# Attention times values: the last three two-head units in 4-value pieces with attn stationary, in a fixed order

The chip is a Trainium2; the kernel runs on one of its cores. The metric is device time in microseconds (us) of one execution, of which several are taken.

## The reference

```python
batch, n_heads, seq, head_dim = 8, 12, 1024, 64
attn_weights: float32 [8, 12, 1024, 1024]
v:            float32 [8, 12, 1024, 64]
out = einsum('bhqs,bhsd->bhqd', attn_weights, v)      # float32
```

The attention matrix is 403 MB and is read once. The matmul contracts over s, which lies along the rows of attn in memory, so each block of attn has to be transposed on the chip first.

## The kernel before

Work is cut into 48 *units* of two heads. A unit's attn sits in one tile of 128 partitions (2 heads x 64) and 16 *values* `g`; one value is 128 rows of attn, 64 queries of each head, with all 1024 keys. Loading converts float32 to bf16. Unit 47 is the last one.

Terms used below: PE is the tensor engine and PEld its loading of the stationary operand, DVE the vector engine, ACT the scalar engine, POOL the GpSimd engine, which issues the loads of attn, SP the sync engine, which issues the stores. The *granted clock* is the share of full speed at which PE runs, 1.00 being full. Tiles: `abf` is attn as loaded, `pt` its transposes, `at` their copy, `vbf` v, `po` the results of wide matmuls, `ot` their copy, `px` the results of direct matmuls, of transposes back and of `spread_v`, `osb` the finished output. In the code, `NP` is 48 units, `G` 16 values, `GH` 8 of them, `HP` 64 queries of a head, `D` 64.

```python
HELD = 7                                   # the last 7 outputs before the last are stored late
LAST = [(0, 3), (3, 3), (6, 3), (9, 3)]
DIRECT = [(12, 2), (14, 1), (15, 1)]
chunks_of = {NP - 2: [(0, GH), (GH, GH)], NP - 1: LAST + DIRECT}   # pieces of the load; else whole
...
def transpose_g(abf, at, g):               # one value: 4 PE transposes of pairs of bf16, seen as fp32
    pt = pt_pool.tile([P, KW, P], fp32)
    ...                                    # then one copy to `at`: DVE for g % 8 in (0,2,4,5,7), else ACT

def multiply(at, vbf, po, h, half, j0, g0, gn):      # v stationary, 512 columns of attn move
    for kw in range(KW):
        for par in range(2):
            nc.tensor.matmul(out=po[h][ds(half * D, D), ds(j0 * HP, gn * HP)],
                             lhsT=vbf[:, 2 * kw + par, h],
                             rhs=at[:, ds(g0, gn), kw, ds(h * HP, HP), par], ...)

def pair(ip):                              # units 0 to 46
    ...
    halves = ip in chunks_of               # only unit 46
    for half in range(2):
        for g in range(half * GH, (half + 1) * GH):
            transpose_g(abf, at, g)
        if halves:
            for h in range(2):
                multiply(at, vbf, po, h, half, 0, half * GH, GH)
    load_ahead(ip)                         # load of unit ip + 2 into this unit's buffer
    if not halves:
        for h in range(2):
            for half in range(2):
                multiply(at, vbf, po, h, half, 0, half * GH, GH)
    to_sbuf(po, ot, 0, GH)                 # the result is [d, q]: it has to be turned back
    ...                                    # even units: spread_v, the v of two later units
    for j0 in (0, 4):
        transpose_back(ot, o_halves, j0, 4)
    ...                                    # store, or hold
```

`last_pair(47)` does the same in pieces of three values, and its last four values (`DIRECT`) the other way round: attn is stationary, both heads' v (128 columns) move, so the result comes out as [q, d] and needs no turning back. Half of what such a matmul computes (a head's queries with the other head's v) is thrown away. `store_held` waits on the sync engine for the load of value 11 and then issues the seven held stores.

An order written in the program is not the order on PE: the compiler's scheduler may move transposes ahead of matmuls.

## Time and profile before

| | before |
|---|---|
| median of 4 runs | 1068.2 us (1065.38 to 1068.39) |
| span of the profiled run | 1066.1 us |
| attn load in the chain of waits | 72% of the span |
| last piece of attn landed (estimate from the medians of the DMA issues) | 1049.8 us |
| last matmul ended | 1062.9 us |

The page of the kernel before: busy time of each engine, the tensor engine's granted clock and the DMA share in tenths for 40 slices, and the chain of waits by engine.

```profile
PE 805.3 (76%) x5438; PEld 639.4 (60%) x5438; DVE 387.4 (36%) x583; ACT 399.8 (38%) x485; POOL 45.3 (4%) x87
...
PEclk9998877888778887888878888888888888888999
DMA  9999999999999999999999999999999999999996
...
DMA 72%; issue 20%; PE 7%; ACT 0%; DVE 0%; POOLq 0%; POOL 0%
```

DMA is full in every slice but the last: loading sets the pace, and computing can gain only in what follows the last loads. That stretch is the end of the chain of waits of the kernel before (start, duration, what):

```profile
1001.57 29.11 DMA abf<-in_attn_weights_dram
1030.68 0.14 issue
1030.81 1.89 PE pt L143 x8
1032.70 4.55 PE po L162 x16
1037.26 4.04 PE pt L143 x32
1041.29 3.73 PE po L162 x16
1045.02 1.52 PE pt L143 x11
...
1061.80 1.08 PE px L273 x16
...
1063.16 0.21 ACT osb L284
```

From 1030.8 us on the chain is PE almost without a gap (pt: transposes, po: wide matmuls, px: direct matmuls or transposes back). Just before, the same kernel by windows of 2 us. After the window and its length, each engine has its busy time and instructions; the last three numbers are the granted clock, the DMA share and GB/s.

```profile
1026.00:1028.00 2.00, 2.00 (x16) 1.84 (x14) 1.48 (x3) 1.73 (x3) 0.00 (x0) 1.00 1.14 239
1028.00:1030.00 2.00, 0.04 (x1) 0.00 (x0) 0.69 (x1) 0.53 (x1) 0.00 (x0) 1.00 0.93 193
1030.00:1032.00 2.00, 1.19 (x6) 1.22 (x7) 0.11 (x1) 0.00 (x0) 0.00 (x0) 0.75 1.06 218
1032.00:1034.00 2.00, 2.00 (x8) 0.92 (x7) 0.58 (x1) 1.01 (x1) 0.00 (x0) 0.50 1.03 212
```

The compiled PE order of the kernel before, from the end of unit 45 on (matmul instructions counted in runs; pxT: transposes back):

```
po 32 | pt 6 | pxT 8 | pt 34 | po 16 | pt 32 | po 16 | pt 11 | ... | px 16
```

PE stands idle for 2.8 us although the first half of unit 46 is transposed and could be multiplied: the scheduler put 6 + 34 transposes, eight of them of the second half, in front of the first 16 wide matmuls (8 pt, then 16 po in the chain), and those eight wait for the load. The clock then drops to 0.50, and 16 wide matmuls take 4.55 us; the next 16 take 3.73.

### The profile page before, as it was taken

The page shows a single profiled execution, that of the slowest core. Times are in us where ns is not written, and L with a number is a line of the kernel's source. Part 1 is how long each engine was busy: PE and PEld are TensorE (multiplying, and loading weights), DVE is VectorE, ACT ScalarE, POOL GpSimd, SP SyncE. Part 2 cuts the span into 40 slices and gives each one's busy share as a digit, 9 for nine tenths or more (in the row PEclk, how much of TensorE's full clock was granted, in tenths as well). Part 3 has the DMA queues.
Part 4 walks back from the last instruction along what each step waited for, and adds up shares of the span by engine and source line. Part 5 has one row for each costly group of instructions (what it writes and reads, how often), then busy time and mean ns, then how long its engine had stood idle before and what let it go on. Part 6 is the DMA issues. An engine that isn't in the chain of part 4 may idle for free.

```text
span 1066.1 us, 12528 instructions
## 1 busy us (share of the span) xinstructions
PE 805.3 (76%) x5438; PEld 639.4 (60%) x5438; DVE 387.4 (36%) x583; ACT 399.8 (38%) x485; POOL 45.3 (4%) x87
## 2 busy tenths in 40 slices
PE   0987668886687767777678776777677876888788
PEld 0675556765566556665566655665467655676667
DVE  0453323443334333443334333343334433343343
ACT  0353324433244333443334333343334433343444
POOL 2000000000000000000000000000000000000010
PEclk9998877888778887888878888888888888888999
DMA  9999999999999999999999999999999999999996
GB/s 216 218 230 229 224 228 231 222 233 229 224 230 224 236 224 224 235 223 224 234 226 225 229 229 227 231 221 234 227 224 233 223 230 229 226 217 217 213 213 207
DMA packets 19062, 240.39 MB, mean 225 GB/s; under 512 B 2112, under 2 KB 2880, under 8 KB 12736
## 3 DMA queue, kind: packets, MB, share of 16 engines
q0 software_dynamic: 11232, 213.39, 93.5%
q1 hardware_dynamic: 7776, 26.22, 6.5%
q8 instruction: 42, 0.69, 0.2%
q14 instruction: 12, 0.10, 0.0%
HBM read 427.82 MB, written 25.17 MB: 425 GB/s over the span
## 4 chain that ended last, share of the span: by engine, by line
DMA 72%; issue 20%; PE 7%; ACT 0%; DVE 0%; POOLq 0%; POOL 0%
DMA abf<-in_attn_weights_dram 72%; PE pt L143 5%; PE po L162 1%; PE px L182 1%; PE px L129 1%; PE px L273 0%; ACT at L152 0%; DVE vbf L137 0%; POOL abf L102 0%; POOLq L102 0%; POOLq L117 0%; DVE osb L284 0%; ACT osb L284 0%; POOLq L72 0%; POOLq L322 0%
## 5 line engine op out<-in xcount | busy, mean ns | idle before, releaser
L143 PE MATMUL pt<-ident,abf 128*128 128x128 f32 x3072 | 453.0, 313 | 221.2 <-DMA abf<-in_attn_weights_dram 221.1
L143 PEld LDWEIGHTS pt<-ident,abf 128*128 128x128 f32 x3072 | 433.9, 213 | 241.4 <-issue 162.5
L152 DVE COPY at<-pt 128x1024 bf16<-128x1024 bf16 x480 | 318.7, 688 | 467.3 <-PE pt L143 465.1
L152 ACT COPY at<-pt 128x1024 bf16<-128x1024 bf16 x288 | 288.3, 1014 | 116.7 <-PE pt L143 116.3
L162 PE MATMUL po<-at,vbf 128*64 128x512 bf16 (+1 forms) x1568 | 236.0, 386 | 0.0
L162 PEld LDWEIGHTS <-vbf 128*64 128x64 bf16 x1568 | 117.8, 108 | 99.8 <-issue 1.2
L190 ACT COPY osb<-px 128x512 f32<-128x512 f32 (+1 forms) x96 | 55.9, 584 | 280.6 <-PE px L182 280.5
L174 ACT COPY ot<-po 128x512 f32<-128x512 f32 (+1 forms) x49 | 28.2, 575 | 200.6 <-PE po L162 200.6
L182 PE MATMUL px<-ident,ot 128*128 128x128 f32 x382 | 86.1, 384 | 17.4 <-DVE vbf L137 17.4
L182 PEld LDWEIGHTS px<-ident,ot 128*128 128x128 f32 x382 | 70.9, 205 | 28.7 <-DVE vbf L137 28.7
L174 DVE COPY ot<-po 128x512 f32<-128x512 f32 (+1 forms) x49 | 33.2, 678 | 105.6 <-PE po L162 105.6
L137 DVE CAST vbf<-px 128x512 bf16<-128x512 f32 x48 | 33.2, 692 | 95.9 <-PE px L129 95.9
L129 PE MATMUL px<-vr,spread 32*128 32x512 bf16 x384 | 53.8, 386 | 18.5 <-DVE vbf L137 18.5
L102 POOL DMA_DIRECT2D abf<-in_attn_weights_dram x55 | 30.2, 554 | 836.1 <-PE pt L143 835.3
L137 ACT CAST vbf<-px 128x512 bf16<-128x512 f32 x48 | 28.1, 586 | 64.0 <-PE px L129 64.0
L129 PEld LDWEIGHTS <-spread 32*128 32x128 bf16 x384 | 17.2, 93 | 52.5 <-issue 43.0
L117 POOL DMA_DIRECT2D vr<-in_v_dram x23 | 12.2, 531 | 140.2 <-PE px L129 140.2
L112 DVE CAST vr<-v 128x2048 bf16<-128x2048 f32 x1 | 1.2, 1228 | 4.4 <-DMA v<-in_v_dram 4.4
L273 PE MATMUL px<-vbf,at 128*128 128x128 bf16 x32 | 2.1, 219 | 0.6 <-ACT at L152 0.6
L84 POOL TENSOR_SCALAR_AFFINE_SELECT spread<-spread 32x512 bf16<-32x512 bf16 x4 | 2.5, 630 | 0.2
L273 PEld LDWEIGHTS <-at 128*128 128x128 bf16 x32 | 1.9, 98 | 0.8 <-ACT at L152 0.8
L137 ACT ACT_TABLE_LOAD x1 | 1.3, 1283 | 0.7 <-PEq L322 0.7
(9 smaller groups left out, 2.5 us busy)
## 6 DMA issues: line engine op xcount, KB each, us to landing
abf<-in_attn_weights_dram POOLq DMA_DIRECT2D x46, 4096.0 KB, 32.9
out_dram<-osb SPq DMA_DIRECT2D x47, 512.0 KB, 19.4
vr<-in_v_dram POOLq DMA_DIRECT2D x23, 512.0 KB, 27.9
abf<-in_attn_weights_dram POOLq DMA_DIRECT2D x2, 2048.0 KB, 23.7
abf<-in_attn_weights_dram POOLq DMA_DIRECT2D x4, 768.0 KB, 20.0
v<-in_v_dram SPq DMA_DIRECT2D x1, 1024.0 KB, 5.0
abf<-in_attn_weights_dram POOLq DMA_DIRECT2D x1, 512.0 KB, 26.7
abf<-in_attn_weights_dram POOLq DMA_DIRECT2D x2, 256.0 KB, 27.7
```

Source lines behind the costliest of these rows:

```text
L84: nc.gpsimd.affine_select(out=spread[ds(h * VP, VP)], in_=spread[ds(h * VP, VP)], compare_op=mybir.AluOpType.not_equal, fill=1.0, base=0, ...
L102: nc.gpsimd.dma_start(out=abf[:, ds(g0, gn)].rearrange("p g s -> p (g s)"), in_=attn_p[ip][:, ds(g0 * S, gn * S)],)
L117: nc.gpsimd.dma_start(out=vr.rearrange("p b x -> p (b x)"), in_=v_g[iv])
L129: nc.tensor.matmul(out=px, lhsT=spread[rows, b], rhs=vr[rows, b], start=(b == 0), stop=(b == VB - 1),)
L137: copy(out=vbf[:, :, h % 2], in_=px.rearrange("p (k d) -> p k d", k=SB))
L143: nc.tensor.matmul(out=pt[:, k], lhsT=words[:, k], rhs=ident, is_transpose=True, start=(k == 0), stop=(k == KW - 1),)
L152: copy(out=at[:, g].rearrange("c k j two -> c (k j two)"), in_=pt.rearrange("c k j -> c (k j)").bitcast(bf16),)
L162: nc.tensor.matmul(out=po[h][ds(half * D, D), ds(j0 * HP, gn * HP)], lhsT=vbf[:, 2 * kw + par, h], rhs=at[:, ds(g0, gn), kw, ds(h * HP, HP ...
L174: copy(out=ot[:, ds(j0, jn), h], in_=po[h][:, ds(j0 * HP, jn * HP)].rearrange("p (j q) -> p j q", j=jn),)
L182: nc.tensor.matmul(out=px[:, j], lhsT=ot[:, j0 + j].rearrange("p h q -> p (h q)"), rhs=ident, is_transpose=True, start=(j == 0), stop=(j = ...
L190: nc.scalar.copy(out=o_halves[:, :, ds(j0, jn)].rearrange("p half j d -> p j half d"), in_=px.rearrange("p j (half d) -> p j half d", half=2),
L273: nc.tensor.matmul(out=px[:, g - g0].rearrange("p h d -> p (h d)"), lhsT=at[:, g, kw, :, par], rhs=vbf[:, 2 * kw + par].rearrange("p h d - ...
```

## The change

The intent is to let PE work on what has landed, with no gap: units 45, 46 and 47 are loaded in pieces, every 4 values are computed by themselves with attn stationary, and the transposes of a piece stand on PE behind the matmuls of the piece before. The diff, cut to its core:

```diff
-    LAST = [(0, 3), (3, 3), (6, 3), (9, 3)]
-    DIRECT = [(12, 2), (14, 1), (15, 1)]
-    chunks_of = {NP - 2: [(0, GH), (GH, GH)], NP - 1: LAST + DIRECT}
+    MARK = 11
+    DG = 4
+    LAST = 3
+    chunks_of = {
+        NP - 3: [(0, GH), (GH, GH)],
+        NP - 2: [(g, DG) for g in range(0, G, DG)],
+        NP - 1: [(0, 4), (4, 4), (8, 4), (12, 2), (14, 1), (15, 1)],
+    }
+    stores_of = {4: (0, 8), 8: (8, 4), 12: (12, 2), 15: (14, 2)}
 ...
+    def direct_pair(ip, behind):
 ...
+        for c0, cn in chunks_of[ip]:
+            for g0 in range(c0, c0 + cn, DG):
+                gn = min(DG, c0 + cn - g0)
+                with tc.issue_after(behind.ins):
+                    for g in range(g0, g0 + gn):
+                        transpose_g(abf, at, g)
+                px = px_pool.tile([P, gn, 2, D], fp32)
+                for g in range(g0, g0 + gn):
+                    n = 0
+                    for kw in range(KW):
+                        for par in range(2):
+                            behind = nc.tensor.matmul(
+                                out=px[:, g - g0].rearrange("p h d -> p (h d)"),
+                                lhsT=at[:, g, kw, :, par],
+                                rhs=vbf[:, 2 * kw + par].rearrange("p h d -> p (h d)"), ...)
+                for h in range(2):
+                    copy = nc.vector.tensor_copy if h == 0 else nc.scalar.copy
+                    rows = ds(h * HP, HP)
+                    copy(out=osb[rows, ds(g0, gn)], in_=px[rows, :, h])
+                ...                      # stores of unit 47 after values 7, 11, 13 and 15
+        load_ahead(ip)
 ...
-    for ip in range(NP - 1):
-        pair(ip)
-    last_pair(NP - 1)
+    for ip in range(NP - LAST):
+        last = pair(ip)
+    for ip in range(NP - LAST, NP):
+        last = direct_pair(ip, last)
```

More of the change, by code (lines that the diff above doesn't have):

```diff
@@ L42 @@
     NV = NH // VH
-    LH = 6
     HELD = 7
-    LAST = [(0, 3), (3, 3), (6, 3), (9, 3)]
-    DIRECT = [(12, 2), (14, 1), (15, 1)]
-    chunks_of = {NP - 2: [(0, GH), (GH, GH)], NP - 1: LAST + DIRECT}
+    MARK = 11
[7 more added lines that the diff above has]
+    stores_of = {4: (0, 8), 8: (8, 4), 12: (12, 2), 15: (14, 2)}
     attn_p = attn_weights.rearrange("b (hp two) (p g) s -> (b hp) (two p) (g s)", two=2, p=HP, g=G)
@@ L155, in transpose_g, with multiply @@
         )
-    def multiply(at, vbf, po, h, half, j0, g0, gn):
+    def multiply(at, vbf, po, h, half):
         n = 0
@@ L162, in multiply @@
                 nc.tensor.matmul(
-                    out=po[h][ds(half * D, D), ds(j0 * HP, gn * HP)],
+                    out=po[h][ds(half * D, D)],
                     lhsT=vbf[:, 2 * kw + par, h],
-                    rhs=at[:, ds(g0, gn), kw, ds(h * HP, HP), par],
+                    rhs=at[:, ds(half * GH, GH), kw, ds(h * HP, HP), par],
                     start=(n == 0),
@@ L169, in multiply, with to_sbuf @@
                 n += 1
-    def to_sbuf(po, ot, j0, jn):
+    def to_sbuf(po, ot):
         for h in range(2):
             copy = nc.vector.tensor_copy if h == 0 else nc.scalar.copy
-            copy(
-                out=ot[:, ds(j0, jn), h],
-                in_=po[h][:, ds(j0 * HP, jn * HP)].rearrange("p (j q) -> p j q", j=jn),
-            )
+            copy(out=ot[:, :, h], in_=po[h].rearrange("p (j q) -> p j q", j=GH))
     def transpose_back(ot, o_halves, j0, jn):
@@ L181, in transpose_back @@
         for j in range(jn):
-            nc.tensor.matmul(
+            last = nc.tensor.matmul(
                 out=px[:, j],
@@ L193, in transpose_back @@
         )
+        return last
     held = {}
@@ L218, in pair @@
         o_halves = osb.rearrange("p (half j) d -> p half j d", half=2)
-        halves = ip in chunks_of
-        for half in range(2):
-            for g in range(half * GH, (half + 1) * GH):
-                transpose_g(abf, at, g)
-            if halves:
-                for h in range(2):
-                    multiply(at, vbf, po, h, half, 0, half * GH, GH)
-        load_ahead(ip)
-        if not halves:
-            for h in range(2):
-                for half in range(2):
-                    multiply(at, vbf, po, h, half, 0, half * GH, GH)
-        to_sbuf(po, ot, 0, GH)
+        for g in range(G):
+            transpose_g(abf, at, g)
+        load_ahead(ip)
+        for h in range(2):
+            for half in range(2):
+                multiply(at, vbf, po, h, half)
+        to_sbuf(po, ot)
         if ip % 2 == 0 and ip // 2 + 1 < NV:
@@ L235, in pair @@
         for j0 in (0, 4):
-            transpose_back(ot, o_halves, j0, 4)
+            last = transpose_back(ot, o_halves, j0, 4)
         if ip < NP - 1 - HELD:
@@ L240, in pair @@
             held[ip] = osb
-    def last_pair(ip):
+        return last
+    def direct_pair(ip, behind):
         abf = abf_of.pop(ip)
@@ L245, in last_pair @@
         vbf = vbf_of.pop(ip)
-        po = [po_pool.tile([P, GH * HP], fp32, name="po") for h in range(2)]
-        ot = ot_pool.tile([P, GH, 2, HP], fp32)
         osb = o_pool.tile([P, G, D], fp32)
-        o_halves = osb[:, : 2 * LH].rearrange("p (half j) d -> p half j d", half=2)
-        out_halves = out_p[ip][:, : 2 * LH].rearrange("p (half j) d -> p half j d", half=2)
-        store_held(abf, 2 * LH - 1)
-        for g0, gn in LAST:
-            for g in range(g0, g0 + gn):
-                transpose_g(abf, at, g)
-            half, j0 = divmod(g0, LH)
-            for h in range(2):
-                multiply(at, vbf, po, h, half, j0, g0, gn)
-            if half:
-                to_sbuf(po, ot, j0, gn)
-                transpose_back(ot, o_halves, j0, gn)
-                nc.sync.dma_start(
-                    out=out_halves[:, :, ds(j0, gn)], in_=o_halves[:, :, ds(j0, gn)]
-                )
@@ L265, in last_pair @@
-        for g0, gn in DIRECT:
-            px = px_pool.tile([P, gn, 2, D], fp32)
-            for g in range(g0, g0 + gn):
-                transpose_g(abf, at, g)
-            for g in range(g0, g0 + gn):
-                n = 0
-                for kw in range(KW):
-                    for par in range(2):
-                        nc.tensor.matmul(
-                            out=px[:, g - g0].rearrange("p h d -> p (h d)"),
-                            lhsT=at[:, g, kw, :, par],
-                            rhs=vbf[:, 2 * kw + par].rearrange("p h d -> p (h d)"),
-                            start=(n == 0),
-                            stop=(n == SB - 1),
-                        )
-                        n += 1
-            for h in range(2):
-                copy = nc.vector.tensor_copy if h == 0 else nc.scalar.copy
-                rows = ds(h * HP, HP)
-                copy(out=osb[rows, ds(g0, gn)], in_=px[rows, :, h])
-            if g0 != 14:
-                first = min(g0, 14)
-                n = g0 + gn - first
-                nc.sync.dma_start(out=out_p[ip][:, ds(first, n)], in_=osb[:, ds(first, n)])
+        if ip == NP - 1:
+            store_held(abf, MARK)
@@ new lines, in direct_pair @@
+        for c0, cn in chunks_of[ip]:
[3 more added lines that the diff above has]
+                    for g in range(g0, g0 + gn):
+                        transpose_g(abf, at, g)
+                px = px_pool.tile([P, gn, 2, D], fp32)
[6 more added lines that the diff above has]
+                                lhsT=at[:, g, kw, :, par],
+                                rhs=vbf[:, 2 * kw + par].rearrange("p h d -> p (h d)"),
+                                start=(n == 0),
+                                stop=(n == SB - 1),
+                            )
+                            n += 1
+                for h in range(2):
+                    copy = nc.vector.tensor_copy if h == 0 else nc.scalar.copy
+                    rows = ds(h * HP, HP)
+                    copy(out=osb[rows, ds(g0, gn)], in_=px[rows, :, h])
+                if ip == NP - 1 and g0 in stores_of:
+                    gs = ds(*stores_of[g0])
+                    nc.sync.dma_start(out=out_p[ip][:, gs], in_=osb[:, gs])
@@ L290, in load_ahead @@
+        load_ahead(ip)
+        if ip < NP - 1:
+            held[ip] = osb
+        return behind
     def load_ahead(ip):
```

## The prediction

> **What bounds the kernel now.** Loading. In the chain of waits 72% of the span is the attn load; DMA stands at 9 in all but the last of the 40 slices. So only what follows the last loads can move. From the DMA issues and the timeline (profiled span 1066.1 us): unit 45's load lands at 1009.7, the halves of unit 46 at 1019.4 and 1030.7, the pieces of unit 47 from 1033.7 to about 1049.8. The last matmul ends at 1062.9, 13 us after the last piece landed; copy and store take 3.2 us more. From 1030.8 on the chain is PE nearly without gaps: a PE backlog.
>
> **Where it comes from.** In unit 46 the first half's matmuls stand behind transposes of the second half, so PE idles 2.8 us (to 1030.8) for a load while it has work, and restarts at a granted clock of 0.63: 16 matmuls of 512 columns take 4.55 us, later 3.73. (The Trainium skill, "TensorE: Matmul & The Clock Gate", Part 1, has the clock at half after an idle window; the 0.63 agrees.) Half by half, 16 cost 3.73 us; unit 45's 32 together take 4.75.
>
> **The change, costed.** Direct matmuls of 128 columns: 16 of the present tail take 0.89 us on the chain, 56 ns each (the same page, "Back-to-back issue gap", gives about 56 warm, isolated), so 0.445 us per value, 7.1 per unit. Transposes stay: 0.49 us per value.
> - Unit 45: adds 7.1, removes 4.75 and about 1.0 (transposes back): +1.3 us.
> - Unit 46: adds 7.1, removes 4.55 + 3.73 + 0.9 and the 2.8 idle: about -5.
> - Unit 47: adds 5.3 for 12 values, removes 4 x 1.49 + 0.66: -1.3; but the last pieces (2, 1, 1) are now strictly serial: transpose, copy (0.69 DVE, 1.01 ACT), matmul: 2.5 + 2.15 + 1.85 us, some 2.8 of it waiting for copies, where about 1.3 shows now.
> The ot and back copies (0.6 us each) leave ACT and DVE; small copies out of px replace them, off the chain.
>
> **Timeline.** Unit 45 starts as before, about 1010.3. A piece of 4 costs 1.96 + 1.78 + 0.1 = 3.84 us; its copies hide behind the per-value order. Eleven pieces: 1052.5. Serial tail 6.6: last matmul 1059.2. Plus 3.2: span 1062.3, 3.8 us less. The last attn load is issued when unit 45's transposes end, about 1024 instead of 1018.5; it still queues behind unit 46's, so the landings should move little, and PE reaches each piece 4 to 7 us after it landed. So only a third or so of the 13 us goes: direct matmuls cost about what they replace; the gain is the idle and the slow clock.
>
> **Predicted: 1064.5 us, 80% range 1060.5 to 1068.5.** Faster by over 2%: 1%; within 2%: 97%; slower by over 2%: 2%.
>
> **What would show it.** Right: no PE wait on attn after 1011; PE continuous to about 1059 at clock 1.0; the pieces' matmuls at 56 ns; last load issued near 1024, landing near 1050; the chain ends transpose, copy, matmul three times. Wrong: matmuls at 65 ns or more (adds 3.5 us and eats the gain); PE waiting for `at` copies inside the 4-pieces; a DMA load in the chain's tail.
>
> **What would make it wrong.** The later issue of the last load letting fast DMA queues run dry, shifting landings and held stores (slower); px buffers or the serial DVE-then-ACT copies stalling each piece; or PE starting unit 45 sooner than I think (faster).

## The result

The change measured 1065.09 us (median of 4 runs, 1063.66 to 1066.28) beside 1068.22 for the kernel before. The ratio is 0.9976, with a 95% interval of 0.9954 to 0.9999. A ratio is the mean time of one kernel's runs over that of the other's of the same rounds, so it isn't quite the ratio of the medians. A second set of six runs gave 1064.62 and a ratio of 0.9981 (told below). The change is faster by about 0.2%, or 2.0 to 2.6 us by the two ratios. The two profiles of the table differ by more, 3.8 us of span, since the kernel before was profiled in one of its slower runs (1068.12) and the change in one of its faster (1064.05).

| | before | after |
|---|---|---|
| profiled span | 1066.1 us | 1062.3 us |
| transposes of unit 45 begin | 1009.7 | 1010.8 |
| last attn load issued | 1018.5 | 1024.4 |
| load of value 11 landed (held stores released) | 1044.7 | 1045.6 |
| last matmul ended | 1062.9 | 1059.1 |
| last copy ended to end of span | 2.7 us | 2.7 us |

The page of the change:

```profile
PE 806.8 (76%) x5640; PEld 648.9 (61%) x5640; DVE 390.1 (37%) x590; ACT 399.0 (38%) x486; POOL 46.3 (4%) x89
...
PEclk9988878888888887888878888778877888878899
DMA  9999999999999999999999999999999999999998
...
DMA 69%; issue 20%; PE 10%; DVE 0%; ACT 0%; POOLq 0%
```

The end of its chain of waits; L148 are the transposes, L259 the direct matmuls, L157 the copies between them:

```profile
1010.83 1.93 PE pt L148 x16
1012.76 1.79 PE px L259 x32
1014.55 1.99 PE pt L148 x16
1016.53 1.79 PE px L259 x32
...
1050.49 1.79 PE px L259 x32
1052.28 0.55 PE pt L148 x4
...
1052.85 0.70 DVE at L157
...
1053.60 1.23 PE px L259 x16
...
1055.46 1.02 ACT at L157
...
1056.53 0.62 PE px L259 x8
...
1057.71 0.70 DVE at L157
...
1058.46 0.64 PE px L259 x8
```

A piece of four values takes 3.78 us (1.99 + 1.79), eleven times over, and no load stands between the pieces. The windows that showed the idle stretch are now full, at full clock:

```profile
1026.00:1028.00 2.00, 2.00 (x22) 1.99 (x21) 1.60 (x3) 1.39 (x3) 1.56 (x3) 1.00 0.89 172
1028.00:1030.00 2.00, 2.00 (x34) 2.00 (x32) 0.42 (x2) 0.91 (x1) 0.00 (x0) 1.00 1.02 201
1030.00:1032.00 2.00, 2.00 (x24) 1.99 (x23) 1.72 (x4) 1.19 (x2) 0.00 (x0) 1.00 1.02 213
1032.00:1034.00 2.00, 2.00 (x32) 2.00 (x30) 0.79 (x3) 0.29 (x2) 0.00 (x0) 1.00 0.99 209
```

The last three pieces are three serial groups of transpose, copy, matmul; PE waits for a copy in each.

### The profile page after: what moved, and what is told of

Its sections match the earlier page's. It is cut to its first block, busy times and chain, and to the rows that moved or that the text cites. A ratio compares the mean times of both kernels' runs of the same rounds, so it can differ in the third digit from the quotient of the medians.

```text
span 1062.3 us, 12938 instructions
## 1 busy us (share of the span) xinstructions
PE 806.8 (76%) x5640; PEld 648.9 (61%) x5640; DVE 390.1 (37%) x590; ACT 399.0 (38%) x486; POOL 46.3 (4%) x89
## 4 chain that ended last, share of the span: by engine, by line
DMA 69%; issue 20%; PE 10%; DVE 0%; ACT 0%; POOLq 0%
DMA abf<-in_attn_weights_dram 69%; PE pt L148 6%; PE px L259 2%; PE px L134 1%; PE px L184 1%; PE po L167 0%; DVE vbf L142 0%; DVE at L157 0%; ACT at L157 0%; DVE osb L270 0%; ACT osb L270 0%; POOLq L107 0%; POOLq L122 0%; POOLq L77 0%; POOLq L312 0%
## 5 line engine op out<-in xcount | busy, mean ns | idle before, releaser
L148 PE MATMUL pt<-ident,abf 128*128 128x128 f32 x3072 | 455.2, 314 | 214.2 <-DMA abf<-in_attn_weights_dram 214.2
L148 PEld LDWEIGHTS pt<-ident,abf 128*128 128x128 f32 x3072 | 436.7, 214 | 232.8 <-issue 157.9
L157 DVE COPY at<-pt 128x1024 bf16<-128x1024 bf16 x480 | 319.0, 688 | 448.9 <-PE pt L148 446.2
L157 ACT COPY at<-pt 128x1024 bf16<-128x1024 bf16 x288 | 288.3, 1013 | 107.4 <-PE pt L148 106.5
L167 PE MATMUL po<-at,vbf 128*64 128x512 bf16 x1440 | 216.5, 391 | 0.0
L167 PEld LDWEIGHTS <-vbf 128*64 128x64 bf16 x1440 | 106.5, 108 | 92.9
L192 ACT COPY osb<-px 128x512 f32<-128x512 f32 x90 | 52.6, 585 | 276.5 <-PE px L184 276.4
L179 ACT COPY ot<-po 128x512 f32<-128x512 f32 x45 | 26.3, 585 | 191.4 <-PE po L167 191.4
L179 DVE COPY ot<-po 128x512 f32<-128x512 f32 x45 | 31.1, 691 | 100.7 <-PE po L167 100.7
L259 PE MATMUL px<-vbf,at 128*128 128x128 bf16 x384 | 23.9, 219 | 2.3 <-ACT at L157 1.2
L259 PEld LDWEIGHTS <-at 128*128 128x128 bf16 x384 | 22.5, 98 | 3.1 <-DVE at L157 1.5
L270 ACT COPY osb<-px 64x256 f32<-64x256 f32 (+2 forms) x14 | 4.7, 336 | 20.6 <-DVE osb L270 20.6
L270 DVE COPY osb<-px 64x256 f32<-64x256 f32 (+2 forms) x14 | 5.3, 378 | 18.4 <-PE px L259 18.4
```

The source lines that it names most:

```text
L148: nc.tensor.matmul(out=pt[:, k], lhsT=words[:, k], rhs=ident, is_transpose=True, start=(k == 0), stop=(k == KW - 1),)
L157: copy(out=at[:, g].rearrange("c k j two -> c (k j two)"), in_=pt.rearrange("c k j -> c (k j)").bitcast(bf16),)
L167: nc.tensor.matmul(out=po[h][ds(half * D, D)], lhsT=vbf[:, 2 * kw + par, h], rhs=at[:, ds(half * GH, GH), kw, ds(h * HP, HP), par], start= ...
L179: copy(out=ot[:, :, h], in_=po[h].rearrange("p (j q) -> p j q", j=GH))
L192: nc.scalar.copy(out=o_halves[:, :, ds(j0, jn)].rearrange("p half j d -> p j half d"), in_=px.rearrange("p j (half d) -> p j half d", half=2),
L259: behind = nc.tensor.matmul(out=px[:, g - g0].rearrange("p h d -> p (h d)"), lhsT=at[:, g, kw, :, par], rhs=vbf[:, 2 * kw + par].rearrange ...
```

## The experiments

Theory A: the gain is unit 46's idle stretch and its slow clock, while the direct form costs PE about what it replaces. Rival B: the gain is the direct form, which needs no transposes back. Rivals C, D and E: the fixed order inside the pieces, the later issue of the last load, the finer loads. All kernels gave the right result unless told otherwise. e1 to e4 ran beside one set of runs of the kernel before (median 1068.11), e6 and e8 to e10 beside another (1068.13), the last three beside a third (1066.96).

### e1: the kernel before, with unit 46's order alone

```diff
-            for g in range(half * GH, (half + 1) * GH):
-                transpose_g(abf, at, g)
+            with tc.issue_after(last.ins) if halves and half else nullcontext():
+                for g in range(half * GH, (half + 1) * GH):
+                    transpose_g(abf, at, g)
             if halves:
                 for h in range(2):
-                    multiply(at, vbf, po, h, half, 0, half * GH, GH)
+                    last = multiply(at, vbf, po, h, half, 0, half * GH, GH)
```

> The kernel before, with one edit: in unit 46 the second half's transposes stand behind the first half's matmuls; no direct matmuls, no other loads. Theory A (the gain of the change is the removed 2.8 us idle and the slow clock in unit 46, while the direct form costs what it replaces): the first half's matmuls start near 1028 at full clock, unit 46's last matmul ends near 1040.3 instead of 1045.0, everything after it shifts by 4 to 5 us because unit 47's pieces have landed, span near 1061.4 to 1062, time 4 to 5 us under before, that is as good as the change or better (ratio 0.9955 to 0.9965). Theory B (the gain is the direct form: no back transposes, no ot copies): within 1 us of before.

Measured: 1065.98 us (1065.01 to 1066.59, 6 runs), ratio 0.9986 (0.9973 to 0.9998). Its chain of waits:

```profile
1010.30 1.11 PE px L183 x4
...
1020.45 4.74 PE po L162 x32
...
1027.00 3.33 PE pt L143 x26
...
1031.10 3.80 PE po L162 x16
1034.90 5.00 PE pt L143 x40
1039.90 3.73 PE po L162 x16
...
1060.40 1.08 PE px L275 x16
```

The idle stretch is cut to under 1 us and the first 16 wide matmuls take 3.80 us. From unit 45's first wide matmul to the end of the last matmul PE takes 41.0 us (1020.45 to 1061.47); the kernel before takes 44.8 (1018.11 to 1062.87). So the stretch is 3.7 us shorter with wide matmuls and transposes back kept, which speaks against B.

But this profile doesn't show that the edit did it, because PE came late. Unit 45's wide matmuls began at 1020.45 instead of 1018.11, and the first half's transposes of unit 46 ended at 1030.3 instead of 1028.0. The second half landed at about 1030.7 in the kernel before, so the old order too would have waited only some 0.4 us. With no slow clock behind it, the old order would have ended unit 46's matmuls near 1043.3 (an estimate from the durations in the two traces: 1030.8 + 1.0 + 3.73 + 4.04 + 3.73); e1 ended them at 1043.6. The edit and the late start are not told apart here. Of the 2.3 us, about 1.3 had been lost by 1010.3, most of it in unit 44's 58 transposes (8.04 us, 7.11 in the kernel before); about 1.1 went right after, where four transposes back at 1010.30 took 1.11 us instead of 0.66. e10 shows what that second loss is. Only one run of e1 has a profile.

The time gained 2.1 us by the medians, neither the 4 to 5 of A (a miss) nor B's less than 1. And e1's lowest run, 1065.01, is not below the lowest of the kernel before beside it, 1064.93.

### e2: the change without the fixed order

```diff
-                with tc.issue_after(behind.ins):
+                with nullcontext():
```

> The change without its fixed order: the issue-after edge of the transposes is taken away. The compiled PE order then differs from the change in only two places: two transposes move ahead of unit 44's last back transposes, and at the end the order is 12 transposes, 8 matmuls, 1 transpose, 16 matmuls, 3 transposes, 8 matmuls instead of three serial groups. Theory A: the fixed order inside the change does nothing for the 4-value pieces and costs about 1.8 us in the last three pieces (waits for copies of 0.3, 1.2 and 0.8 us go under other work): span near 1060.5. If the stores, which keep the DMA full to 1058 in the change, bind first, only 0.5 to 1 us. Rival C (the fixed order is what gained): 2 us or more slower than the change.

Measured: 1063.73 us (1063.51 to 1064.56, 5 runs), ratio 0.9967 (0.9955 to 0.9980). Rival C falls: without the fixed order nothing is lost. The compiled PE order had already suggested it: in the 4-value pieces it is the same (16 transposes, 32 matmuls, and so on) with the edge or without; only the end differs:

```
change: pt 16 | px 32 | pt 8 | px 16 | pt 4 | px 8 | pt 4 | px 8
e2:     pt 16 | px 32 | pt 12 | px 8 | pt 1 | px 16 | pt 3 | px 8
```

In the profile PE is 1.7 us sooner, its last copy ends at 1057.9 (the change: 1059.6). Yet the span is 1062.2, as good as unchanged: 4.3 us pass from the last copy to the end instead of 2.7. The stores wait, in the sync engine's waits of e2 (total, times, longest) and its last windows:

```profile
SPq L323 <- DMA out_dram<-osb: 2.3, 3, 1.5
```

```profile
1056.00:1058.00 2.00, 0.62 (x8) 0.45 (x8) 0.91 (x2) 0.28 (x2) 0.00 (x0) 1.00 1.01 396
1058.00:1060.00 2.00, 0.00 (x0) 0.00 (x0) 0.00 (x0) 0.00 (x0) 0.00 (x0) 0.77 0.50 180
```

PE has nothing more to do after 1058, but DMA is full up to there and half busy in the two microseconds after. The medians do differ, 1063.73 beside 1065.09 and 1064.62 of the change, while the lowest runs agree (1063.51 and 1063.50): none of e2's five runs is as slow as the slower ones of the change. Whether that is chance, or a late PE is hidden behind the stores there, is not shown.

### e9 and e10: two of the seven held stores left out

e9 is e2, e10 is the change, each with this edit; two outputs are never written, so the result is wrong.

```diff
         with tc.issue_after(waits.ins):
+            held.pop(NP - 1 - HELD)
+            held.pop(NP - HELD)
             for ip in sorted(held):
```

> Wrong on purpose: the kernel of e2 (free order) with two of the seven held outputs never stored, so 1 MB of late stores is gone. Theory F (in e2 PE ended 1.7 us sooner than in the change, and the gain was lost to the stores, which keep the DMA full until 1058 and land the last piece late): the last store lands right behind the last copy again, span 2.7 us after the last copy ends (in e2 it was 4.3 us), so span near 1060.6 and time 1 to 1.5 us under e2 (near 1062.4). Rival G (the end is fixed by something else than the stores' bytes): span stays at 1062.2, the gap stays near 4.3 us.

> Wrong on purpose: the change with two of the seven held outputs never stored. The change's last store issued just as the stores' backlog ended (gap from last copy to end 2.7 us, no more than in the kernel before). Theory F: nothing gained, within 0.5 us of the change. Rival G2 (the stores' bytes slow the whole tail, loads included): 1 us or more faster than the change.

e9 measured 1062.19 us (1061.82 to 1062.35, 5 runs), ratio 0.9949 (0.9936 to 0.9962), 1.5 us under e2. The DMA is free sooner:

```profile
1054.00:1056.00 2.00, 1.67 (x21) 1.31 (x20) 0.75 (x3) 1.10 (x3) 0.00 (x0) 1.00 0.74 280
1056.00:1058.00 2.00, 0.62 (x8) 0.45 (x8) 0.66 (x2) 0.21 (x1) 0.00 (x0) 1.00 0.22 74
```

From the last copy (1057.6) to the end (1060.5) it is 2.9 us again. e10 measured 1064.74 us (1063.79 to 1066.03, 6 runs), ratio 0.9972 (0.9957 to 0.9987): as the change. So in the profiled runs PE still ends last in the change, the stores' backlog stands right behind it, and most of the 1.7 us of PE time that the free order saves is eaten by that backlog. The pair shows it: fewer stores help e2 and not the change. (The runs stand on different chips, but every run of e9, at most 1062.35, lies below every run of e2, at least 1063.51.)

e10's profile fell among its slower runs (1065.99), and shows what sets them apart. Its windows near 1010, and then those of the change:

```profile
1008.00:1010.00 2.00, 1.05 (x8) 0.36 (x7) 0.89 (x2) 0.74 (x2) 0.00 (x0) 0.92 1.00 205
1010.00:1012.00 2.00, 1.94 (x9) 1.94 (x10) 0.01 (x1) 0.58 (x1) 0.00 (x0) 0.50 1.06 221
1012.00:1014.00 2.00, 2.00 (x15) 2.00 (x14) 0.69 (x1) 1.02 (x2) 0.00 (x0) 0.73 1.04 221
```

```profile
1010.00:1012.00 2.00, 2.00 (x20) 2.00 (x19) 0.60 (x1) 1.20 (x3) 0.00 (x0) 1.00 1.06 221
1012.00:1014.00 2.00, 2.00 (x33) 1.99 (x32) 0.78 (x2) 1.81 (x2) 0.00 (x0) 1.00 0.99 209
```

In e10 the clock falls to 0.50 after unit 44's `spread_v` and its waits for copies. From there on both kernels run the same course, and PE ends 1.7 us later (last copy at 1061.3 instead of 1059.6); 0.3 us of that had been lost before (1010.06 against 1009.73 for the transposes back), 1.4 are the slow clock. e10's six runs lie in two groups, 1063.8 to 1063.9 and 1065.6 to 1066.0. The same instructions meet this stretch at full clock in one run and at half in another, and the two profiles differ by about the distance of the groups. That each run of the slower group has it is inferred, not shown.

### e3: only the last two units in the new form

```diff
-    LAST = 3
+    LAST = 2
     chunks_of = {
-        NP - 3: [(0, GH), (GH, GH)],
```

> The change with only the last two units in the new form; unit 45 as before, whole load. Theory A: a unit with its 32 wide matmuls together (4.75 us) and transposes back (1.06) is 1.3 us cheaper than a direct one (7.2), so PE reaches the end 1.3 to 1.7 us sooner; the last load is issued near 1018.5 again, and landings stay: span near 1060.6 to 1061. Rival B (direct form gains in each unit): slower than the change by 1 us or more. Rival D (the late issue of the last load in the change shifts its landings): the piece that the held stores wait for lands 1 us or more sooner than in the change (1045.6).

Measured: 1063.48 us (1063.18 to 1065.07, 6 runs), ratio 0.9968 (0.9955 to 0.9980). Unit 47 begins at 1039.9 us, where the change has 1041.0; 0.4 us of that is a sooner start of unit 45. The rest, 0.6, is what unit 45 saves in the old form: less than the expected 1.3, because its transposes back wait for the copy of `po` (0.6 us). Rival B is wrong for unit 45. The load of value 11 landed at 1045.1, in the change at 1045.6, less than the 1 us that rival D asks for. And PE could not have felt more: in the change it never waits for attn after 1010.

### e4: the change with the coarser loads of before

```diff
-        NP - 3: [(0, GH), (GH, GH)],
-        NP - 2: [(g, DG) for g in range(0, G, DG)],
+        NP - 3: [(0, G)],
+        NP - 2: [(0, GH), (GH, GH)],
```

> The change with the loads of unit 45 in one piece and of unit 46 in two, as before; the computing and its order are unchanged. Theory A: PE comes to every piece of these two units 0.8 us or more after it landed, so nothing is lost: same as the change within 1 us. Rival E (the finer loads are part of the gain): 2 us or more slower than the change, with PE waiting for attn after 1010.

Measured: 1064.10 us (1063.87 to 1064.23, 5 runs), ratio 0.9969 (0.9957 to 0.9981): as the change, and no PE wait for attn after 1010 us. Rival E falls; the finer loads of units 45 and 46 do nothing.

### e8: only the last unit in the new form

`LAST = 1`; unit 46 is loaded in halves, does all its transposes, then its 32 wide matmuls together.

> Only the last unit in the new form; unit 46 does all its transposes, then its 32 wide matmuls together. Theory A: PE waits some 2.8 us for the second half of unit 46 (1030.7), but the wide matmuls cost 4.75 instead of 7.2 us and nothing of this unit stands in the wrong order, so unit 47 begins near 1039.5 to 1040.5, as in e3 (1039.9): time within 1 us of e3. Rival B (unit 46 needs the direct form in 4-value pieces): 2 us or more slower than e3, near the kernel before.

Measured: 1065.04 us (1063.96 to 1066.21, 5 runs), ratio 0.9977 (0.9963 to 0.9992), 1.6 us above e3: a miss. Its chain of waits:

```profile
1030.66 5.56 PE pt L147 x32
1036.22 4.76 PE po L166 x32
...
1041.04 0.59 ACT ot L178
...
1042.78 1.92 PE pt L147 x16
```

Two of its windows, PE idle and then the slow clock:

```profile
1028.00:1030.00 2.00, 0.00 (x0) 0.00 (x0) 0.62 (x1) 0.37 (x1) 0.00 (x0) 1.00 0.96 201
1032.00:1034.00 2.00, 2.00 (x12) 2.00 (x11) 0.82 (x2) 1.02 (x2) 0.00 (x0) 0.50 1.06 221
```

Unit 47 begins at 1042.8, 2.9 us later than in e3. The expectation left out that PE, after the wait for the second half, restarts at half clock: 32 transposes take 5.56 us, where 16 at full clock take 1.99 (1.6 us lost). The copy ahead of the transposes back is 0.6 more. So in the profiles unit 46 does profit from the piecewise form: not since its matmuls are cheaper than 32 wide ones together, but since PE is never without work there. By the times alone this is not clear of noise: e8 and e3 ran on different chips, and their intervals overlap.

One thing more is in these numbers. e8 keeps the idle stretch and the slow clock, and yet its times can't be told from those of the change (1065.04 beside 1065.09 and 1064.62; ratios 0.9977 beside 0.9976 and 0.9981). Its 32 wide matmuls together take 4.76 us where the two sixteens of the kernel before take 8.28 (4.55 at the slow clock, 3.73 at full). So there was a second cost in unit 46, multiplying half by half, and a kernel that sheds this cost but keeps the idle stretch measures about as fast. In the profiles e8's last matmul ends at 1060.9, between the change (1059.1) and the kernel before (1062.9).

### e6 and e11: the best of these together

e6 is e3 without the fixed order (e3's and e2's edits); e11 is e6 with `HELD = 6`.

> Only the last two units in the new form, and no fixed order (e3 and e2 together). PE alone would end about 2.4 us sooner than in the change (1.8 from the free tail, 0.6 from unit 45). Theory F: the stores bind, so span not below about 1061, and time 1062.7 to 1063.5, as e3 and e2 or barely better. Rival G: span near 1059.8, time near 1061.5.

> The kernel of e6 with six outputs held back instead of seven; the result is right. Theory F (in e6 the stores' backlog binds): 0.5 MB less of late stores, some 1.2 us less DMA after the loads, but the loads land as much later; PE reached unit 45 just as it landed, so PE shifts by up to 1.2 us and the end by 0 to minus 0.8 us: 1062.2 to 1063. Rival G (stores don't bind): 0.5 to 1.2 us slower than e6, since only the loads move.

e6 measured 1062.95 us (1062.79 to 1063.50, 5 runs), ratio 0.9957 (0.9944 to 0.9971): below the kernel before, and its median is below every run of the change (lowest 1063.50). PE's last copy ends at 1056.5, 3.0 us sooner than in the change, but the span is 1061.7, with 5.2 us behind the last copy: the stores bind, as e2 and e9 say. e11 measured 1063.14 us (1062.69 to 1064.51, 6 runs), ratio 0.9966 (0.9953 to 0.9979), no better. Its profile fell on a run with the slow clock at 1012 (1064.51), so it doesn't tell the two theories apart; inconclusive.

### Second looks: the change and the kernel before

> The change itself, unaltered, beside the next two on one chip. Expected 1063.7 to 1066.3 as in its first four runs, in two groups about 2.2 us apart: the slower group is the one in which the profile shows a clock of 0.5 near 1010 us (seen in the slow profiles of e1 and e10, absent in the others).

> The kernel before, unaltered, for a second profile. Its times fall in two groups (about 1065 and 1068.2). If this profile falls in the fast group, the clock after the 2.8 us idle of unit 46 should not drop to half, or the idle should be missing; if in the slow group, both are there as in the first profile.

The change again: 1064.62 us (1063.50 to 1066.72, 6 runs), ratio 0.9981 (0.9966 to 0.9997). Not two clean groups this time: three runs lie between. Its profile (a run of 1063.72) was at full clock near 1010, so it doesn't test what the slower runs have. It tells something else: PE is about 1.0 us sooner than in the first profile of the change (last copy ended at 1058.6 instead of 1059.6), yet the span is 1062.0, only 0.3 us shorter, with 3.4 us behind the last copy. The same program shows what e2 shows: PE time saved there hardly counts. The kernel before, in one run with a profile: 1068.17 us, with the idle stretch (to 1030.8) and 5.15 us for the 16 wide matmuls behind it. Both profiles of the kernel before are thus of its slower runs; why some of its runs take about 1065 us stays open.

## Why the prediction was right

- *Loading bounds the kernel, only the tail can move.* Held: DMA stays full, the share of the load in the chain went from 72% to 69%.
- *A piece of four costs 3.84 us, eleven pieces end at 1052.5, the last matmul at 1059.2, the span is 1062.3.* The profile: 3.78 us, 1052.28, 1059.1, 1062.3. The time, 1064.5 predicted, was 1065.09 in the first set and 1064.62 in the second. That the span agrees to 0.1 us is in part luck: PE began 0.5 us later than thought and the tail took 0.2 us longer, the pieces were 0.8 us shorter in all, and the profile fell on a run at full clock; a run like e10's ends nearly 2 us later. The gain forecast was 3.7 us; the ratios make it 2.0 to 2.6.
- *Unit by unit +1.3, -5 and about +0.2 us* (for unit 47: -1.3 for the matmuls, +1.5 for the waits in the tail). From the two traces, counting each unit from the end of the one before and putting transposes that were moved across back to their own unit: unit 45 about +1.4, unit 46 about -5.9, unit 47 about +0.2. So the gain is in unit 46, as predicted. Of its 5.9 us, 2.8 are the idle stretch and 1.7 the slow clock (8 transposes in 1.89 us instead of 1.0, half of what 16 take at full clock, 16 matmuls in 4.55 instead of 3.73); most of the rest is that direct matmuls (7.2) are cheaper than wide ones half by half with their transposes back (8.4 at full clock). This is a reckoning from two traces, estimates in part. Against 32 wide matmuls together the direct form saves nothing (e3).
- *Direct matmuls at 56 ns.* 32 in 1.79 us are 56 ns each. The Trainium skill ("TensorE: Matmul & The Clock Gate", "Back-to-back issue gap") gives about 56 ns for an isolated warm matmul of 128 columns and about 81 for a stream of weight load and matmul pairs; this stream of pairs ran at 56.
- *The last load's later issue does no harm.* Held: issued at 1024.4, value 11 landed 0.9 us later, PE didn't wait.
- What the prediction did not see: the stores. It called PE the end of the chain, which was true by a margin of little more than nothing; in the profiles the next 1.7 us of PE time are worth almost none (e2, e9, and the second profile of the change). It also took the clock to be 1.0 from 1010 on, which is so in some runs only.
- What stays open: how the gain splits between e1's order and the rest of the change. e1's interval (0.9973 to 0.9998) and the change's (0.9966 to 0.9997 in its second set) overlap. e1's profile doesn't isolate the order, and the times of e8, which keeps the idle stretch, can't be told from the change's. So that the idle stretch and the slow clock make most of the gain is read from the traces; no experiment isolates it. Nor was it tested whether the new sizes of unit 47's four stores (256, 128, 64 and 64 KB instead of 192, 192, 64 and 64) matter.

## What to carry to other kernels

In a kernel bound by loading, look for the stretch behind the last load, and there for an engine that idles with ready work behind an instruction that waits: compare the compiled order with the program's, since the scheduler may have put it there. A change of the matmul's form can pay by keeping PE fed although, over the units that it touches, it saves hardly any PE time. Before crediting a shorter stretch in a trace to an edit, check that the engine entered it at the same time: an engine that comes late waits less for the same load. And before shortening the last engine further, look at what ends just behind it; here the held stores had been invisible, and took most of the next 1.7 us.

## What the Trainium skill lacked or had wrong

- "TensorE: Matmul & The Clock Gate", the rule against idle gaps over about 3 us between bursts ("Why this matters for your kernels"), is not enough by itself here: in e10 the clock fell to 0.50 at 1010 us although no gap in the 4 us before was over 0.8 us; PE was busy 1.49 and 1.05 of 2 us in these windows, with matmuls of 32 rows. The change went through the same instructions at 1.00. (The page's section "A second HAM failure mode: psum-queue depth-cycling" does tell of frequent short idles that lower the clock, but gives no length for them.)
- The same page, Part 4, says that the clock doesn't go up for transposes. Here it does: 6 transposes of 128x128 float32 took 1.53 us at a clock of 0.5 (at 990.5 us in the kernel before), and after that, with nothing but transposes on PE, 58 took 7.11 us, 123 ns each, at a clock of 1.0.
- The same page, "Back-to-back issue gap", has about 81 ns per pair of weight load and matmul at 128 columns; the pieces of the change ran at 56 ns per pair over eleven stretches of 32.
- No page that was used says how much the completion of a small store grows behind a backlog on the same engines: the last 64 KB stores took 1.6 us from issue to landing in the kernel before and 3.9 us (median of two) in e2.
